# A hybrid attention and state-space layer on one core: the sample's scan chunk padded to 128 rows, its index heads taken in pairs

## The chip, the cores and the metric

The kernel runs on one core of a Trainium2 chip. The metric is device time in microseconds (us) of one execution, lower is better. A core has five engines that run their own instruction lists: TensorE (PE in the profile, with PEld for its weight loads), VectorE (DVE), ScalarE (ACT), GpSimd (POOL) and SyncE (SP), whose queue issues the transfers between main memory and on-chip memory. On-chip memory has 128 partitions ("rows" below); matmul results go to accumulator banks, which ScalarE and VectorE read out.

## What is computed

One layer of a streaming encoder, for a prompt of 512 tokens and a sample of 64 tokens with a cache of 512 keys. Both share all weights, so the kernel treats them as 576 tokens. Cut to what the change touches:

```python
# light indexer: scores over the keys, 8 heads, top k keys per query (sample: 144 of 576)
logits = einsum('thd,sd->ths', q_idx, k_idx) * 64 ** -0.5
score  = einsum('th,ths->ts', w, relu(logits))
idx    = top_k(score, k)            # attention then runs over these keys alone

# Mamba-2 scan, 32 heads in 8 groups, per chunk of tokens
decay  = exp(where(causal, acs_i - acs_j, -inf))
y_diag = einsum('ijg,ijgr,jgr,jgrp->igrp', cc @ bc, decay, dt, x)
y_off  = einsum('ign,igr,grpn->igrp', cc, exp(acs), h_prev)
y      = y_diag + y_off
```

Around this stand the conditioning (adaLN), one input projection, softmax attention over the chosen keys, a causal convolution, gates, an output projection and a SwiGLU feed-forward part.

## The kernel before

**How it is written and ordered.** The whole layer is recorded as a list of operations: each call on `pe`, `vec`, `act`, `pool` or `sync` becomes an `Op` of a `Plan` (line 229), with its reads and writes as dependences. `Plan.cost` (line 316) gives each operation a price, and `Plan.order` (line 363) simulates the five engines with these prices and a fixed delay between engines; whichever operation is ready first, by price and by place in the list, is put next into its engine's list. The order on every engine is therefore the result of the prices, and a changed price or a new operation can move others. All instructions are issued by one helper, so each has line 490 in the profile; tiles tell them apart. On the chip each engine works through its list strictly in order and waits with semaphores.

For a matmul the price depends on its form. Matmuls on rounded float32 (`F32R`) cost about their columns divided by 2.25 per ns; a plain float32 matmul has another price; and one with a `tile_position`, which places a 64- or 32-column weight tile in a part of the array, has (line 337)

```python
return (73 if o.shape[0] <= 32 else 8 + n) / 1e3, 0.10
```

with `n` the columns of the streamed operand.

**Precision.** Most products split both operands in a rounded high part and a rest (`wh`, `wl` of the weights, `hTh`, `hTl` of the activations) and add three matmuls. ScalarE rounds the weights (`wh`), VectorE forms the rest (`wl`). A plain float32 matmul, such as those of the scan, shows as two records in the profile.

**Stages.** Conditioning and normalization (about the first 80 us), input projection with the index part (80 to 260 us, lines 963 to 1118), attention of four key heads filled up with further columns of the projection (260 to 490), convolution and scan of eight groups interleaved with the last columns of the projection (490 to 850), branch projections with the rest of the conditioning (850 to 1010), output projection and feed-forward part (to the end).

**The index part (lines 1090 to 1118).** Block `b == 4` is the sample. Its queries lie in `qis` behind those of the prompt, head by head, 64 columns each; the weights of the heads lie in `wi`. For each of eight heads and each half of the 576 keys two matmuls (high part and rest of the keys `kis`) give `pix` in 64 rows, ScalarE applies the relu into a tile tagged `lg`, and VectorE multiplies by the head's weight and adds to `score4`. Then 18 rounds of `max` and `match_replace` on VectorE find the top 144 keys. Blocks 1 to 3 are the prompt's, with 128 rows.

**The scan (lines 1262 to 1311).** `chunk(g, c, xb, st)` computes chunk `c` of group `g`: chunks 0 to 3 are 128 prompt tokens each, chunk 4 is the 64 sample tokens. `bc` is loaded with the summed decay, GpSimd masks it into `dec`, ScalarE takes four exponentials, VectorE multiplies by `pc`, TensorE transposes the inputs, VectorE forms `xdt` and `xw`. Then, for each of four heads `h`,

```python
pe.matmul(o, xdt[:L, 64 * h:64 * h + 64], dec[:L, h, :L], start=True, stop=st is None,
          tile_position=(0, 64 * (h % 2)))
pe.matmul(o, st[:, 64 * h:64 * h + 64], cs[:, h, :L], start=False, stop=True,
          tile_position=(0, 64 * (h % 2)))
```

The first contracts over the `L` tokens of the chunk (64 for the sample), the second over the 128 state columns (`cs` is the decayed C, `st` the state). A further matmul of `xw` and `bt` gives the new state. `dec`, `xdt` and `xw` each have two buffers used in turn. `stage_a` (line 1327) is one projection tile (48 matmuls) and its convolution with the buffers `xc`, `cu` and `cth`; `stage_b` calls `chunk`, and for the sample it loads the state (`si`) first; `stage_c` normalizes a group. The loop at line 1383 interleaves them, and lets the conditioning's last two parts (`adr`, line 674) run in the last group.

**Memory.** Pools are opened and closed in a stack. The pools of the scan (`ssd`, line 1237, and `conv`, line 1239) take the place of attention's (`attn`, `attn2`), which hold among others the split probabilities `pth`, `ptl`, the copy `otmp` of an attention result (line 1175) and the sum `oT` (line 1226). The first write to a new tile waits for the last use of every old tile that lay there.

Of the kernel before, what the change touches and what calls it, by code (L numbers as in the profile page):

```python
# [5 lines left out]
F32 = mybir.dt.float32  # L6
# [7 lines left out]
P = 128  # L14
# [214 lines left out]
class Plan:  # L229
# [86 lines left out]
    def cost(self, op, outs, ins):  # L316
        e, fn = op.eng, op.fn
        o = outs[0] if outs else None
        if e == "sync":
            v = o if o is not None else ins[0]  # L320
            n = 4
            for k in v.shape:
                n *= k
            op.bytes = n
            return 0.06, 0.93
        n = _cols(o)
        if e == "tensor":
            op.mm = True
            if fn == "transpose":
                return 0.110, 0.10  # L330
            rhs = op.args[2]
            fast = rhs.dtype == F32R
            n = _cols(rhs)
            if fast:
                return (n / 2.25 + 4 if n > 128 else 110) / 1e3, 0.10
            if op.kw.get("tile_position") is not None:
                return (73 if o.shape[0] <= 32 else 8 + n) / 1e3, 0.10
            return ((4 * max(n, 128) / 2.4 if n > 1 else 190) + 5) / 1e3, 0.10
        psum = any(is_psum(v) for v in ins)
        if e == "scalar":  # L340
            t = n / 1.2 + (52 if psum else 92) + (96 if isinstance(op.kw.get("bias"), View) else 0)
            return (t + (93 if op.kw.get("accum_out") is not None else 0)) / 1e3, 0.19
        if e == "vector":
            if fn == "tensor_reduce":
                n = _cols(ins[0])
            if fn in ("max", "match_replace"):
                n = _cols(ins[0] if fn == "max" else o)
            if fn == "reciprocal":
                return (69 + 6.25 * n) / 1e3, 0.13
            src = sum(1 for v in ins if _cols(v) > 1)  # L350
            fast = src == 1 and fn in ("tensor_copy", "tensor_scalar") and not is_psum(o) and not psum
            column = fn in ("scalar_tensor_tensor", "tensor_scalar") and len(ins) > src
            more = 60 * column + 70 * (fn == "tensor_tensor_reduce")
            return (64 + 0.96 * more + n * (0.5 if fast else 1.0)) / 0.96e3, 0.13
        if fn == "memset":
            return (n * 0.5 + 60) / 1e3, 0.1
        if op.kw.get("op") == OP.pow or OP.pow in op.args:
            return (n * 165 + 300) / 1e3, 0.1
        per = {"tensor_copy": 3.33, "affine_select": 1.0, "tensor_tensor": 2.1}[fn]
        return (n * per + 150) / 1e3, 0.1  # L360
# [137 lines left out]
def build(tc, I, O):  # L498
# [476 lines left out]
    vec.tensor_copy(misc[:NS, 4, :], p[:NS, :104])  # L975
    wi = cp.tile([P, 5, 8], F32, name="wi")
    vec.tensor_scalar(wi, misc[:, :, 64:72], float(NIH ** -0.5), None, op0=OP.mult)

    ki = misc[:, :, 0:64]
    rope("ki", ki, cs2, 1, False)  # L980
# [109 lines left out]
    for b in (4, 1, 2, 3):  # L1090
        smp = b == 4
        n = T if smp else P * (b + 1)
        rows = NS if smp else P
        k0 = NP_ if smp else 0
        s = ix.tile([P, n], F32, name=f"score{b}")
        for h in range(NIH):
            q0 = 8 * NP_ + h * NS if smp else h * NP_ + b * P
            q = qis[:, q0:q0 + rows]
            for c0, cn in (((0, TH), (TH, TH)) if smp else ((0, n),)):
                ps = px(f"pix{b}_{h}_{c0}", "py")  # L1100
                for a in range(2):
                    pe.matmul(ps[:rows, :cn], q, kis[:, a, k0 + c0:k0 + c0 + cn], start=(a == 0), stop=(a == 1))
                r = ap_.tile([P, NP_], F32, name=f"relu{b}_{h}_{c0}", tag="lg", bufs=4)
                sv = s[:rows, c0:c0 + cn]
                act.activation(r[:rows, :cn], ps[:rows, :cn], AF.Relu, scale=float(HD ** -0.5))
                if h == 0:
                    vec.tensor_scalar(sv, r[:rows, :cn], wi[:rows, b, h:h + 1], None, op0=OP.mult)
                else:
                    vec.scalar_tensor_tensor(sv, r[:rows, :cn], wi[:rows, b, h:h + 1], sv, op0=OP.mult, op1=OP.add)
        if not smp:  # L1110
            pool.memset(s[0:64, n - 64:n], -1.0e38)
        m8 = ix.tile([P, 8], F32, name=f"m8_{b}")
        for r in range((TOPK_S if smp else TOPK_P) // 8):
            vec.max(m8[:rows], s[:rows, :n])
            vec.match_replace(s[:rows, :n], m8[:rows], s[:rows, :n], -3.0e38)
        vec.tensor_scalar(masks[b][:rows], s[:rows, :n], -2.0e38, NEG, op0=OP.is_gt, op1=OP.mult)
        if smp:
            vec.tensor_copy(masks[b][64:128], masks[b][0:64])
# [143 lines left out]
    def chunk(g, c, xb, st):  # L1262

        L = P if c < 4 else NS
        i0 = c * P
        nm = f"s{g}_{c}"
        h4 = lambda z: z[:L].rearrange("p (h d) -> p h d", h=4)
        bc = sd.tile([P, 4, P], F32, name=nm + "bc", tag="bc", bufs=2)
        sync.dma_start(bc[:, :, :L], acs_d[4 * g:4 * g + 4, i0:i0 + L][None].to_broadcast([P, 4, L]))
        dec = sd.tile([P, 4, P], F32, name=nm + "dec", tag="dec", bufs=2)  # L1270
        pool.affine_select(dec[:L, :, :L], bc[:L, :, :L], pattern=[[0, 4], [1, L]], compare_op=OP.is_ge, fill=NEG,
                           base=0, channel_multiplier=-1)
        for h in range(4):
            act.activation(dec[:L, h, :L], dec[:L, h, :L], AF.Exp, bias=nacs[:L, c, 4 * g + h:4 * g + h + 1])
        pt = px(nm + "xt")
        pc = pt[:, 384:512]
        pe.matmul(pc[:L, :L], xb[:, 2, i0:i0 + L], xb[:, 3, i0:i0 + L], start=True, stop=True)
        vec.tensor_tensor(dec[:L, :, :L], dec[:L, :, :L], pc[:L, None, :L].to_broadcast([L, 4, L]), OP.mult)
        for i in range(3):
            pe.transpose(pt[:L, P * i:P * i + P], xb[:, i, i0:i0 + L], ident)  # L1280
        xdt = sd.tile([P, 256], F32, name=nm + "xdt", tag="xdt", bufs=2)
        xw = sd.tile([P, 256], F32, name=nm + "xw", tag="xw", bufs=2)
        bt = sd.tile([P, P], F32, name=nm + "bt", tag="bt", bufs=2)
        for o, s in ((xdt, dtp), (xw, wst)):
            vec.tensor_tensor(h4(o), h4(pt[:, 0:256]), s[:L, c, 4 * g:4 * g + 4, None].to_broadcast([L, 4, HD]), OP.mult)
        act.activation(bt[:L], pt[:L, 256:384], AF.Copy)
        if st is not None:
            cs = sd.tile([P, 4, P], F32, name=nm + "cs", tag="cs", bufs=1)
            act.activation(bc[:, :, :L], bc[:, :, :L], AF.Exp)
            pool.tensor_tensor(cs[:, :, :L], bc[:, :, :L], xb[:, None, 3, i0:i0 + L].to_broadcast([P, 4, L]), OP.mult)  # L1290
        py = px(nm + "y", "py")
        for h in range(4):
            o = py[64 * (h % 2):64 * (h % 2) + 64, P * (h // 2):P * (h // 2) + L]
            pe.matmul(o, xdt[:L, 64 * h:64 * h + 64], dec[:L, h, :L], start=True, stop=st is None,
                      tile_position=(0, 64 * (h % 2)))
            if st is not None:
                pe.matmul(o, st[:, 64 * h:64 * h + 64], cs[:, h, :L], start=False, stop=True,
                          tile_position=(0, 64 * (h % 2)))
        ps = py[:, 256:512]
        pe.matmul(ps, bt[:L], xw[:L], start=True, stop=True)  # L1300
        new = sd.tile([P, 256], F32, name=nm + "h", tag="hst", bufs=4)
        if st is None:
            act.activation(new, ps, AF.Copy)
        else:
            pool.tensor_tensor(new.rearrange("p (h d) -> p h d", h=4), st.rearrange("p (h d) -> p h d", h=4),
                               edec[:, c, 4 * g:4 * g + 4, None].to_broadcast([P, 4, HD]), OP.mult)
            vec.tensor_tensor(new, new, ps, OP.add)
        for i in range(2):
            vec.scalar_tensor_tensor(xb[:, i, i0:i0 + L], xb[:, i, i0:i0 + L], dcol[:, 2 * g + i:2 * g + i + 1],
                                     py[:, P * i:P * i + L], op0=OP.mult, op1=OP.add)  # L1310
        return new
# [10 lines left out]
    so_p = O["ssm_prompt"][0, 0].rearrange("h p n -> (h p) n").rearrange("(g a p) n -> g p a n", a=2, p=P)  # L1322
    so_s = O["ssm_sample"][0, 0].rearrange("h p n -> (h p) n").rearrange("(g a p) n -> g p a n", a=2, p=P)

    xbs, sts = {}, {}

    def stage_a(g, i):
# [443 lines left out]
```

## Time and profile before

| what | value |
|---|---|
| median of 3 runs | 1446.85 us (1444.67 to 1447.4) |
| the profiled execution, whole | 1454.0 us |
| its span, first to last instruction | 1452.3 us |
| mean granted TensorE clock | 0.993 |
| TensorE busy, of the span | 1415.3 us |
| VectorE busy | 1078.2 us |
| ScalarE busy | 705.2 us |
| GpSimd busy | 211.1 us |
| moved by transfers | 179.73 MB |

The profile is of one execution. Lines of the timeline read: start in us, duration in us, engine, source line, operation, output tile <- input tiles, then for TensorE rows of contraction * columns of weights, then the output's partitions x elements, and xN for N merged instructions; in brackets stands the idle time ahead and who ended it. Rows of groups end in "busy us, mean ns of one | idle us before, and who ended it". Rows of stages give for each engine the busy time and in brackets the instructions, then the granted clock of TensorE, the share of busy transfer engines and GB/s. TensorE's matmuls are pipelined: their durations overlap, and what one costs is seen from the next one's start.

### The profile page before, as it was taken

Reading aid. Unit: us, or ns where it says so; the run is one execution under the profiler, and the core shown is the slowest. Engines: PE = TensorE matmul, PEld = TensorE weight load, DVE = VectorE, ACT = ScalarE, POOL = GpSimd, SP = SyncE. Lnnn points to the kernel's source line nnn. Section 1 sums busy time; section 2 is a strip of 40 time slices with the busy share of each in tenths; the row PEclk is TensorE's granted clock in tenths of the full one; section 3 lists DMA queues with packets and bytes.
Section 4 is the critical chain, followed back from the end, with each engine's and each line's share of the span. In section 5 each row is a group of like instructions: output and inputs, shape, how many; then the busy total and the mean of one; then the engine's idle time right before and its main releaser. Section 6 shows DMA issues by size and latency. Waiting matters only on the chain.

```text
span 1452.3 us, 27797 instructions
## 1 busy us (share of the span) xinstructions
PE 1415.3 (97%) x10865; PEld 1339.4 (92%) x10865; DVE 1078.2 (74%) x2123; ACT 705.2 (49%) x1482; POOL 211.1 (15%) x320
## 2 busy tenths in 40 slices
PE   7999999999999899999999899999999999999998
PEld 5889999999999699999998699999999999999998
DVE  4468999887877777778777578984699888874221
ACT  5335233556556656555555441123566666663221
POOL 1211001210200144444444210000000000000000
PEclk9999999999999999999999999999999999999999
DMA  9822346333332434344333857775513333324331
GB/s 281 227 73 76 84 112 163 94 84 89 109 92 77 129 99 108 100 112 111 84 88 96 280 171 238 230 229 170 165 44 102 88 99 92 102 70 137 112 107 28
DMA packets 262356, 179.73 MB, mean 124 GB/s; under 512 B 24272, under 2 KB 239472, under 8 KB 262224
## 3 DMA queue, kind: packets, MB, share of 16 engines
q1 hardware_dynamic: 262224, 177.95, 42.7%
q8 instruction: 85, 1.39, 0.4%
q14 instruction: 47, 0.39, 0.1%
HBM read 153.09 MB, written 24.83 MB: 123 GB/s over the span
## 4 chain that ended last, share of the span: by engine, by line
PE 84%; DVE 8%; DMA 5%; SPq 1%; ACT 1%; issue 1%; DVEq 0%; ACTq 0%
PE mm L490 60%; PE py L490 15%; PE px L490 8%; DMA adr<-in_w_ada 2%; DMA raw<-in_w_in 2%; DVE aacc L490 1%; SPq L490 1%; DVE wl L490 1%; DVE m L490 1%; DVE score L490 1%; DMA xt<-in_x_sample 1%; ACT wh L490 0%; DMA x2r<-x_d 0%; DVE P L490 0%; DVE e L490 0%
## 5 line engine op out<-in xcount | busy, mean ns | idle before, releaser
L490 ACT ACTIVATE wh<-raw 128x1024 fp32r<-128x1024 f32 (+2 forms) x159 | 156.6, 987 | 279.9 <-PE mm L490 222.4
L490 DVE TENSOR_TENSOR wl<-raw,wh 128x1024 fp32r<-128x1024 f32 (+1 forms) x137 | 169.0, 1236 | 100.6 <-ACT wh L490 97.8
L490 PE MATMUL mm<-hTl,wh 128*128 128x288 f32 (+1 forms) x1024 | 235.0, 304 | 0.0
L490 PE MATMUL mm<-hTh,wh 128*128 128x288 f32 (+1 forms) x1024 | 230.6, 302 | 1.7 <-ACT xc L490 1.5
L490 PE MATMUL mm<-hTh,wl 128*128 128x288 f32 (+1 forms) x1024 | 232.1, 301 | 0.0
L490 PEld LDWEIGHTS mm<-hTh,wh 128*128 128x128 f32 (+1 forms) x1024 | 166.7, 189 | 5.4 <-ACT xc L490 1.8
L490 PEld LDWEIGHTS mm<-hTl,wh 128*128 128x128 f32 (+1 forms) x1024 | 167.4, 189 | 4.0 <-issue 1.9
L490 PEld LDWEIGHTS mm<-hTh,wl 128*128 128x128 f32 (+1 forms) x1024 | 167.3, 189 | 2.7 <-issue 0.5
L490 DVE SCALAR_TENSOR_TENSOR cu<-xc,wc,cu 128x579 f32<-128x579 f32 x96 | 82.9, 868 | 4.0 <-ACT cu L490 3.5
L490 PE MATMUL mm<-fl,wh 128*128 128x288 f32 x352 | 80.6, 298 | 1.0 <-DVE fl L490 1.0
L490 PE MATMUL mm<-fh,wl 128*128 128x288 f32 x352 | 80.1, 298 | 0.9 <-DVE x2r L490 0.9
L490 PE MATMUL mm<-fh,wh 128*128 128x288 f32 x352 | 80.0, 297 | 0.0
L490 PE MATMUL mm<-wh,hTl 128*128 128x256 f32 x256 | 73.2, 286 | 0.0
L490 PE MATMUL mm<-wh,hTh 128*128 128x256 f32 x256 | 72.8, 286 | 0.0
L490 PE MATMUL mm<-wl,hTh 128*128 128x256 f32 x256 | 72.7, 284 | 0.0
L490 DVE SCALAR_TENSOR_TENSOR aacc<-adr,sil,aacc 128x512 f32<-128x512 f32 x84 | 58.7, 747 | 2.9 <-DMA adr<-in_w_ada 2.7
L490 ACT ACTIVATE P<-lg,mn 128x128 f32<-128x128 f32 (+4 forms) x72 | 41.8, 582 | 39.1 <-DVE mn L490 38.3
L490 PEld LDWEIGHTS mm<-fh,wl 128*128 128x128 f32 x352 | 58.2, 189 | 1.6 <-DVE x2r L490 1.4
L490 PEld LDWEIGHTS mm<-fl,wh 128*128 128x128 f32 x352 | 58.2, 189 | 1.6 <-DVE fl L490 1.4
L490 PEld LDWEIGHTS mm<-fh,wh 128*128 128x128 f32 x352 | 58.1, 189 | 0.1
L490 PE MATMUL mm<-yh,wl 128*128 128x288 f32 x256 | 56.8, 302 | 0.0
L490 PE MATMUL mm<-yh,wh 128*128 128x288 f32 x256 | 56.5, 300 | 0.0
(409 smaller groups left out, 3771.0 us busy)
## 6 DMA issues: line engine op xcount, KB each, us to landing
raw<-in_w_in SPq DMA_DIRECT2D x80, 512.0 KB, 4.2
adr<-in_w_ada SPq DMA_DIRECT2D x48, 512.0 KB, 5.2
rawu<-in_w_gate_up SPq DMA_DIRECT2D x22, 512.0 KB, 3.9
raw<-in_w_gate_up SPq DMA_DIRECT2D x22, 512.0 KB, 3.9
bc<-acs_d SPq DMA_DIRECT2D x32, 256.0 KB, 3.6
raw<-in_w_branch_ssm SPq DMA_DIRECT2D x16, 512.0 KB, 4.9
raw<-in_w_down SPq DMA_DIRECT2D x16, 512.0 KB, 3.7
gate_d<-sg SPq DMA_DIRECT2D x16, 288.0 KB, 4.8
```

The source lines that it names most:

```text
L490: getattr(engines[x.eng], x.fn)(*[real(a) for a in x.args], **{k: real(v) for k, v in x.kw.items()})
```

## The change

Three things are changed. The index part computes the sample's heads two at a time: the 64 columns of two neighbouring heads are one weight tile of 128 columns, so that even heads are summed in rows 0 to 63 of `score4` and odd heads in rows 64 to 127; a small tile `wi2` holds the head weights in that layout, and at the end ScalarE copies the odd half down and VectorE adds it. In the scan, the sample's chunk has `dec` and `xdt` tiles of its own, `decS` and `xdtS`, one buffer each, whose rows 64 to 127 are set to zero once at the start; the first of the two matmuls per head contracts over all 128 rows. The planner's price for matmuls with a `tile_position` and more than 32 columns of weights becomes 132 ns, whatever the streamed columns.

```diff
-                return (73 if o.shape[0] <= 32 else 8 + n) / 1e3, 0.10
+                return (73 if o.shape[0] <= 32 else 132) / 1e3, 0.10
...
+    wi2 = cp.tile([P, 4], F32, name="wi2")
+    for r in range(2):
+        vec.tensor_copy(wi2[64 * r:64 * r + 64], wi[0:NS, 4].rearrange("p (b r) -> p r b", r=2)[:, r])
...
-        for h in range(NIH):
-            q0 = 8 * NP_ + h * NS if smp else h * NP_ + b * P
-            q = qis[:, q0:q0 + rows]
+        for h in range(NIH // 2 if smp else NIH):
+            q0 = 8 * NP_ + h * P if smp else h * NP_ + b * P
+            q = qis[:, q0:q0 + P]
+            w1 = wi2[:, h:h + 1] if smp else wi[:, b, h:h + 1]
...
-                    pe.matmul(ps[:rows, :cn], q, kis[:, a, k0 + c0:k0 + c0 + cn], start=(a == 0), stop=(a == 1))
+                    pe.matmul(ps[:, :cn], q, kis[:, a, k0 + c0:k0 + c0 + cn], start=(a == 0), stop=(a == 1))
...
-        if not smp:
+        if smp:
+            odd = ap_.tile([P, T], F32, name="odd", tag="lg", bufs=4)
+            act.activation(odd[0:NS], s[NS:P, :], AF.Copy)
+            vec.tensor_tensor(s[0:NS, :], s[0:NS, :], odd[0:NS], OP.add)
+        else:
             pool.memset(s[0:64, n - 64:n], -1.0e38)
...
-        dec = sd.tile([P, 4, P], F32, name=nm + "dec", tag="dec", bufs=2)
+        dec = decS if c == 4 else sd.tile([P, 4, P], F32, name=nm + "dec", tag="dec", bufs=2)
...
-        xdt = sd.tile([P, 256], F32, name=nm + "xdt", tag="xdt", bufs=2)
+        xdt = xdtS if c == 4 else sd.tile([P, 256], F32, name=nm + "xdt", tag="xdt", bufs=2)
...
-            pe.matmul(o, xdt[:L, 64 * h:64 * h + 64], dec[:L, h, :L], start=True, stop=st is None,
+            pe.matmul(o, xdt[:, 64 * h:64 * h + 64], dec[:, h, :L], start=True, stop=st is None,
...
+    decS = sd.tile([P, 4, NS], F32, name="decS")
+    xdtS = sd.tile([P, 256], F32, name="xdtS")
+    pool.memset(decS[NS:P], 0.0)
+    pool.memset(xdtS[NS:P], 0.0)
```

The relu and the multiply-and-add of the index part work on 128 rows instead of 64 for the sample; all else is as before.

More of the change, by code (lines that the diff above doesn't have):

```diff
@@ L1101, in build @@
                 for a in range(2):
-                    pe.matmul(ps[:rows, :cn], q, kis[:, a, k0 + c0:k0 + c0 + cn], start=(a == 0), stop=(a == 1))
+                    pe.matmul(ps[:, :cn], q, kis[:, a, k0 + c0:k0 + c0 + cn], start=(a == 0), stop=(a == 1))
                 r = ap_.tile([P, NP_], F32, name=f"relu{b}_{h}_{c0}", tag="lg", bufs=4)
-                sv = s[:rows, c0:c0 + cn]
-                act.activation(r[:rows, :cn], ps[:rows, :cn], AF.Relu, scale=float(HD ** -0.5))
+                sv = s[:, c0:c0 + cn]
+                act.activation(r[:, :cn], ps[:, :cn], AF.Relu, scale=float(HD ** -0.5))
                 if h == 0:
-                    vec.tensor_scalar(sv, r[:rows, :cn], wi[:rows, b, h:h + 1], None, op0=OP.mult)
+                    vec.tensor_scalar(sv, r[:, :cn], w1, None, op0=OP.mult)
                 else:
-                    vec.scalar_tensor_tensor(sv, r[:rows, :cn], wi[:rows, b, h:h + 1], sv, op0=OP.mult, op1=OP.add)
-        if not smp:
+                    vec.scalar_tensor_tensor(sv, r[:, :cn], w1, sv, op0=OP.mult, op1=OP.add)
+        if smp:
[3 more added lines that the diff above has]
+        else:
             pool.memset(s[0:64, n - 64:n], -1.0e38)
```

## The prediction

> **What bounds the kernel now.** I read the first page from its top down, then a table of stages, then the waits of TensorE, and only then single instructions. The page says who is busy and what the chain that ended last is made of:
>
> ```profile
> span 1452.3 us, 27797 instructions
> ...
> PE 1415.3 (97%) x10865; PEld 1339.4 (92%) x10865; DVE 1078.2 (74%) x2123; ACT 705.2 (49%) x1482; POOL 211.1 (15%) x320
> ...
> PE 84%; DVE 8%; DMA 5%; SPq 1%; ACT 1%; issue 1%; DVEq 0%; ACTq 0%
> ```
>
> TensorE is busy for 97% of the span and holds 84% of the chain. An average can hide stages with other limits, so the next view cuts the span at the places that the change touches: the sample's index matmuls (110 to 126 us), the top-k after them (126 to 254), the end of attention (480 to 500), the scan (500 to 798), and the wait for data behind it (798 to 812).
>
> ```profile
> core 0: us, PE busy (x) PEld busy (x) DVE busy (x) ACT busy (x) POOL busy (x), PEclk, DMA share, GB/s
> 110.00:126.00 16.00, 16.00 (x128) 15.51 (x128) 13.93 (x29) 12.98 (x31) 1.54 (x1) 1.00 0.24 66
> 126.00:254.00 128.00, 127.67 (x970) 126.50 (x968) 123.73 (x270) 43.67 (x68) 9.62 (x7) 1.00 0.42 115
> 480.00:500.00 20.00, 16.75 (x76) 12.69 (x75) 14.19 (x29) 11.09 (x25) 1.94 (x13) 0.83 0.24 70
> 500.00:798.00 298.00, 297.82 (x2340) 269.66 (x2339) 232.56 (x446) 174.77 (x427) 134.06 (x229) 1.00 0.40 106
> 798.00:812.00 14.00, 9.71 (x93) 6.86 (x91) 7.28 (x12) 4.39 (x7) 1.70 (x2) 0.88 0.91 289
> ```
>
> In both stages that lose work TensorE never rests: 16.00 of 16 us and 297.82 of 298. VectorE is nearly as full behind the index scores (123.73 of 128) and has room in the scan (232.56 of 298). All that TensorE waited for in the scan, by the view of waits cut to 500 to 798 us, is one line:
>
> ```profile
> PE px L490 <- DVE dec L490: 0.2, 1, 0.2
> ```
>
> So a microsecond less of TensorE work in these stages is nearly a microsecond less of kernel, as long as nobody else becomes late.
>
> **The index part.** The sample had eight heads times two halves of the keys times two operand parts: 32 matmuls with 64 columns of weights. Two heads at a time make 16 with 128 columns. Their price is read from the timeline of TensorE, by starts, since the durations overlap:
>
> ```profile
> 112.90 0.43 PE L490 MATMUL py<-kis,qis 128*64 128x288 f32 x2
> 113.17 0.28 PE L490 MATMUL mm<-wh,hsS 128*128 128x256 f32 x1
> ```
>
> Two of them move the next matmul 0.27 us on, 0.135 us each. With 288 columns streamed in either form, 16 fewer are 16 x 0.135 = **2.2 us less TensorE work**. On VectorE eight of sixteen score operations go, and an addition over 576 columns and two small copies of head weights come. The nearest rows of the groups by shape are
>
> ```profile
> L490 DVE SCALAR_TENSOR_TENSOR score<-lg,wi,score 64x288 f32<-64x288 f32 x14 | 6.4, 507 | 0.6 <-ACT lg L490 0.6
> L490 DVE TENSOR_TENSOR m<-m,g 128x576 f32<-128x576 f32 x8 | 6.0, 755 | 0.0
> L490 DVE COPY misc<-px 64x104 f32<-64x104 f32 x1 | 0.2, 246 | 0.0
> ```
>
> which makes -8 x 0.507 + 0.755 + 2 x 0.246 = -2.8 us (128 rows instead of 64 are taken to cost the same time: a row is its own lane). VectorE, the other full engine of this stage, thus sheds as much as TensorE, and the end of the stage moves forward whichever of the two carries it. The new wait is a chain of last score, copy of the odd half on ScalarE, addition on VectorE. In the changed program's order VectorE has a score operation of the next block on each side of the addition, and ScalarE, 43.67 us busy of 128 in that stage, has evacuations behind its copy; TensorE has other products for all of that time; the chain of work shows one unbroken stretch of them:
>
> ```profile
> 190.96 62.78 PE mm L490 x471
> ```
>
> I take the new chain at nothing; with no cover it would cost about 1.5 us once (two operations of some 0.75 us).
>
> **The scan part.** This is the bigger term. The sample's chunk issues, per group, eight float32 matmuls with a column position, alternately `dec`/`xdt` with 64 rows of contraction and `cs`/state with 128 rows. Each appears as two records:
>
> ```profile
> 526.35 0.42 PE L490 MATMUL mm<-hTl,wh 128*128 128x288 f32 x2
> 526.61 0.43 PE L490 MATMUL mm<-hTh,wl 128*128 128x288 f32 x2
> 526.97 0.32 PE L490 MATMUL py<-dec,xdt 64*64 64x64 f32 x2
> 527.23 0.33 PE L490 MATMUL py<-cs,hst 128*64 128x64 f32 x2
> 527.48 0.33 PE L490 MATMUL py<-dec,xdt 64*64 64x64 f32 x2
> ...
> 529.02 0.70 PE L490 MATMUL py<-xw,bt 64*128 64x256 f32 x2
> ```
>
> From 526.97 to 529.02 the eight take 2.05 us: every change between 64 and 128 rows moves the next start by 0.26 us. A prompt chunk issues the same eight with 128 rows throughout and twice the columns:
>
> ```profile
> 535.12 0.45 PE L490 MATMUL py<-dec,xdt 128*64 128x128 f32 x4
> 535.39 0.40 PE L490 MATMUL py<-cs,hst 128*64 128x128 f32 x4
> 535.61 0.44 PE L490 MATMUL py<-dec,xdt 128*64 128x128 f32 x4
> 535.82 0.44 PE L490 MATMUL py<-cs,hst 128*64 128x128 f32 x4
> 536.19 0.70 PE L490 MATMUL py<-xw,bt 128*128 128x256 f32 x2
> ```
>
> 1.07 us for sixteen records, half of the sample's time for twice its columns. Padding the sample's contraction with zero rows puts all eight in the prompt's form, so 1.07 us bounds the new block from above. The lower end comes from one pair without a change in it, and the time of one load:
>
> ```profile
> L490 PEld LDWEIGHTS py<-dec,xdt x320: 129/136/137, 520.4 to 842.4; 128*64 128x64 f32 x128, 64*64 64x64 f32 x32
> 526.97 0.19 PEld L490 LDWEIGHTS py<-dec,xdt 64*64 64x64 f32 x2 [0.17 <-DVE xw L490]
> ```
>
> Two loads of 0.136 us span 0.19 us, so the second starts 0.054 us after the first. With twice the columns a record takes 0.108 us; sixteen in two column halves that run beside each other are 8 x 0.108 = 0.86 us, and 0.21 us of the prompt's 1.07 is entry and exit. The same with 0.054 gives 8 x 0.054 + 0.21 = 0.64 us. Between 0.64 and 1.07 I take the middle, 0.85: half the columns must shorten something, but the weights that each record loads are the prompt's. A group then saves 1.2 us (0.98 to 1.41), and eight groups **9.6 us** (7.8 to 11.3). The `xw`/`bt` matmul keeps its 64 rows; its own entry and exit stay as they are. VectorE, with 65 us free in this stage, loses nothing by the shorter block.
>
> Here a rule speaks against the change. The Trainium skill, "TensorE: Matmul & The Clock Gate", Part 3, "What overlaps and what doesn't", says that a weight load overlaps matmuls in flight only when its row group differs; after padding all eight share all rows. The trace differs: it shows 1.07 us for sixteen records in one row group, where load and stream one after the other would need 16 x 0.108 = 1.73 us even with 64 columns.
>
> **What the change moves besides.** Two tiles of 1 KB per partition at the head of the scan's pool push the convolution's input buffers 2 KB up. In the built programs the first of them, `xc`, lay on attention's probability splits; it now lies also on `otmp`, which the last `oT` addition reads. Today the first evacuation into `xc` begins at 492.76, before that addition ends, and the second one waits for it:
>
> ```profile
> 492.76 0.78 ACT L490 ACTIVATE xc<-mm 128x288 f32<-128x288 f32 x3
> 493.71 0.78 ACT L490 ACTIVATE xc<-mm 128x288 f32<-128x288 f32 x3 [0.17 <-DVE oT L490]
> 492.77 0.85 DVE L490 TENSOR_TENSOR oT<-py,otmp 64x256 f32<-64x256 f32 x2 [1.21 <-ACT otmp L490]
> 493.59 0.85 PE L490 MATMUL mm<-hTh,wh 128*128 128x288 f32 x2 [1.48 <-ACT xc L490]
> ```
>
> TensorE waits 1.48 us for that first evacuation. In the changed program both evacuations wait for `oT`, so the first starts when the second does now: 493.71 - 492.76 = **0.95 us more idle TensorE**, once (0 at best, if the addition is done sooner; some 2 at worst, if the pause prolongs the stretch of lower clock, 0.83 in this window). The cover it loses is real: nothing else is queued on TensorE ahead of that accumulator. The two zero fills stand on GpSimd ahead of the convolution's fills and wait for tiles long read; GpSimd is idle there. `decS` and `xdtS` take the sample out of the two-buffer rings of `dec` and `xdt`, which can only release GpSimd's selections earlier.
>
> The planner's own price for these matmuls (72 to 132 ns with 64 columns) and the new operations make it lay out the order anew from the index part on. The lists of SyncE differ only by transfers that change places with near neighbours. After the scan TensorE still stands before the same load:
>
> ```profile
> 807.33 1.08 PE L490 MATMUL py<-adr,sil 128*32 128x128 f32 x16 [2.99 <-DMA adr<-in_w_ada]
> ```
>
> That load is issued when earlier matmuls of TensorE free its buffer, and the window's other loads when the last `hTh` matmul has run, so this stall moves forward with TensorE and neither grows nor shrinks; I count 0, with 1 us either way.
>
> **The sum** is -2.2 - 9.6 + 0.95 = -10.9 us (rounded). The profiled execution took 1454.0 us, 1.7 of them outside its span of 1452.3; from it the changed kernel would take 1443.1. It stands 7.15 us above the median of the three runs, 1446.85, and the forecast goes by that median: 1446.85 - 10.9 = **1436.0 us**.
>
> **The rivals.**
>
> *The loads are not hidden.* If a weight load does wait for the matmuls in flight of its rows, a record costs load plus stream, 0.054 + 0.054 us, the block 1.73 us, and a group saves 0.32: -2.2 - 8 x 0.32 + 0.95 = -3.8, 1443.0 us. For it: no row shows eight 64-column matmuls in a row with 128 rows. Against it: the prompt's 1.07 us. This is the time that the quoted rule of the Trainium skill gives.
>
> *The change does not do what it says.* The 0.26 us per pair could belong to short matmuls that add into the same accumulator, not to the change of rows. Then only the index part and the seam count: -1.25 us, 1445.6 us, which cannot be told from no change. Against it: the pair within one operation adds into the same accumulator too, and moves on after 0.054 us.
>
> *Slower: ScalarE is blocked in the scan.* In the changed order ScalarE's four exponentials on `decS` and that on `bc` stand earlier than before, ahead of weight roundings and of the evacuations of TensorE's accumulators; they wait, by way of GpSimd's selection, for the sample's `bc` load. TensorE has two accumulators, and one product is 48 matmuls of 0.13 us (the two rows at 526.35 and 526.61), 6.4 us. So a blocked ScalarE costs nothing up to 6.4 us and every microsecond beyond it stops TensorE. It turns the sign from 10.9 / 8 = 1.4 us beyond that, at blocks of 7.8 us per group; blocks of 9 us would give -10.9 + 8 x 2.6 = +9.9, 1456.8 us. For it: the order is laid out anew, and no row shows the new one. Against it: ScalarE is busy 174.77 of 298 us, and the load lands in less than that by far:
>
> ```profile
> bc<-acs_d SPq DMA_DIRECT2D x32, 256.0 KB, 3.6
> ```
>
> **How the numbers follow.** Forecast 0.70, loads not hidden 0.08, no effect of the rows 0.07, slower 0.12; 0.03 is left for gains beyond the forecast's own ends. Those ends are, with the block at 0.64 us, no cost at the seam and 1 us less stall behind the scan, -2.2 - 11.3 - 1 = -14.5 (1432.4), and with the block at 1.07, 2 at the seam and 1 us more stall, -2.2 - 7.8 + 3 = -7.0 (1439.9). The range runs from 1431.5, a little below the first, for the runs' own spread, to 1443.5, which takes in the rival of the loads; it holds some 0.79. Faster or slower means by more than 0.2%, 2.9 us, about what a measurement of this kernel tells from no change: faster 0.81, same 0.07, slower 0.12.
>
> **What would show it.** In the profile after, 16 rows `kis`/`qis` with 128x288; in each group the start of `xw`/`bt` or of the next product 0.64 to 1.07 us after the first `decS`/`xdtS`, and no step of 0.26 us between pairs. TensorE's wait for `xc` near 490 us should be about 2.4 us. Wrong would be: a block near 1.7 or 2.05 us; waits of TensorE for ScalarE inside the scan; or a shorter scan whose gain is found again as a longer wait for `adr`.

## The result and the profile after

The changed kernel takes **1434.0 us** (median of four runs, 1431.16 to 1435.6) beside 1446.68 for the kernel before (four runs, 1444.67 to 1447.4): a ratio of 0.9912, 95% interval 0.9893 to 0.9932, 12.7 us less. The forecast was 1436.0 (10.9 less), with a range of 1431.5 to 1443.5. A second comparison on another occasion, told below, gave 0.9898 (0.9881 to 0.9915), again with a median of 1434.0.

The first page of the changed kernel's profile, the lines that answer to those of before (busy times, and the chain that ended last):

```profile
span 1433.3 us, 27708 instructions
...
PE 1396.6 (97%) x10849; PEld 1326.3 (93%) x10849; DVE 1081.6 (75%) x2118; ACT 702.6 (49%) x1475; POOL 217.7 (15%) x322
...
PE 86%; DVE 7%; DMA 3%; ACT 1%; issue 1%; SPq 1%; POOL 0%; ACTq 0%; DVEq 0%
```

The span fell by 19.0 us and TensorE's busy time by 1415.3 - 1396.6 = 18.7. Its idle time is 36.7 us after 37.0, but these are not the same waits: ahead of the first index matmul it fell from 16.4 to 12.9 us, and in the stages behind that it rose by 3.2 in sum (0.6 in the index stage, 0.9 at the seam, 1.2 in the scan, 0.8 at the end, and 0.3 less in the others together). TensorE still holds the chain.

19.0 is more than the 12.7 of the medians, so a part of it belongs to the two executions and not to the change. To find it, the span is cut at instructions that both kernels have (differences of their starts in the timeline of TensorE, us). Beside the two first profiles stands a second one of each kernel, told below (TensorE busy 1413.5 and 1398.7 us, idle 34.1 and 34.3):

```
stage (first to last)                     before  again   after   again
start to the first index matmul           112.90  108.05  107.09  108.03
first to last index matmul                 77.42   77.43   75.10   75.09
to the last product of attention (ptl)    301.29  301.27  301.13  301.48
seam, to the scan's first px<-xb           23.92   23.45   25.22   25.21
scan, to the last px<-ident,rows          335.60  335.76  325.62  324.79
branches, to the first mm<-mh             141.39  141.64  139.66  139.14
to the first feed-forward mm<-fh          302.21  302.18  302.20  302.24
to the last mm<-fh,wh                     152.13  152.38  151.09  151.06
to the end                                  5.44    5.44    6.19    6.06
```

Most stages repeat within 0.3 us; the changed kernel's scan and branches and before's seam differ by 0.5 to 0.8. Only the first one is off by more, and it holds the same work in the same order in both kernels: before's first execution spent 4.85 us more there than its second, 3.4 of them as idle time of TensorE. That is why the forecast did well to go by the median and not by the profiled execution. Taking means of the two columns, the change gives -2.3 (index), +1.5 (seam), -10.5 (scan), -2.1 (branches), -1.2 (feed-forward) and +0.7 (end): -13.9 us, of the size of the measured 12.7 and 13.9.

*Index.* The matmuls' row in the view of the tile, and one pair in the timeline of TensorE:

```profile
L490 PE MATMUL py<-kis,qis x64: 274/334/497, 107.1 to 182.4; 128*128 128x288 f32 x16, 128*128 128x256 f32 x16, 128*128 128x384 f32 x16, 128*128 128x512 f32 x16
```

```profile
113.84 0.42 PE L490 MATMUL py<-kis,qis 128*128 128x288 f32 x2
114.10 0.28 PE L490 MATMUL mm<-wl,hTh 128*128 128x256 f32 x1
```

Sixteen of 288 columns where there were 32, and two of them still move the next one on by 0.26 us. TensorE's idle time in this stage is 1.0 us after 0.3: a wait of 0.3 us for VectorE's `wl` and a second one as long for ScalarE's `lg` are new.

*Scan.* The sample's block of one group, in the timeline of TensorE, and the weight loads of the same block:

```profile
600.82 0.29 PE L490 MATMUL mm<-hTl,wh 128*128 128x288 f32 x1
601.04 0.34 PE L490 MATMUL py<-decS,xdtS 128*64 128x64 f32 x4
601.20 0.29 PE L490 MATMUL py<-cs,hst 128*64 128x64 f32 x4
601.32 0.33 PE L490 MATMUL py<-decS,xdtS 128*64 128x64 f32 x4
601.43 0.33 PE L490 MATMUL py<-cs,hst 128*64 128x64 f32 x4
601.70 0.70 PE L490 MATMUL py<-xw,bt 64*128 64x256 f32 x2
602.33 0.49 PE L490 MATMUL px<-xb 128*128 128x128 f32 x2
```

```profile
601.03 0.20 PEld L490 LDWEIGHTS py<-decS,xdtS 128*64 128x64 f32 x4 [0.16 <-issue]
601.14 0.21 PEld L490 LDWEIGHTS py<-cs,hst 128*64 128x64 f32 x4
601.26 0.25 PEld L490 LDWEIGHTS py<-decS,xdtS 128*64 128x64 f32 x4
601.38 0.25 PEld L490 LDWEIGHTS py<-cs,hst 128*64 128x64 f32 x4
```

The block lasts 601.70 - 601.04 = 0.66 us, in all eight groups 0.66 or 0.67, where it lasted 2.05 or 2.06. A step of four records takes 0.11 to 0.16 us; only the last one, ahead of another form of tile, takes 0.27. The loads keep the matmuls' pace.

*What TensorE waits for in the scan* (view of waits, 498 to 860 us), and the two loads behind it in the timeline:

```profile
PE py L490 <- DMA adr<-in_w_ada: 4.0, 2, 3.0
PE mm L490 <- ACT oh L490: 1.5, 1, 1.5
```

```profile
790.68 0.65 PE L490 MATMUL py<-adr,sil 128*32 128x128 f32 x16 [3.00 <-DMA adr<-in_w_ada]
813.52 0.64 PE L490 MATMUL py<-adr,sil 128*32 128x128 f32 x16 [1.04 <-DMA adr<-in_w_ada]
```

No wait for ScalarE but the one for `oh` at the end, 1.30 us before and 1.5 now. The stall at `adr` is 3.00 us after 2.99, and a second one of 1.04 us is new (0.67 in the second profile, whose first one is 2.58).

*Seam.* TensorE's first matmul after its wait, ScalarE's first evacuation, and two rows from the slower stretch that follows:

```profile
486.25 0.53 PE L490 MATMUL mm<-hTh,wh 128*128 128x288 f32 x2 [2.43 <-ACT xc L490]
...
488.10 0.68 PE L490 MATMUL mm<-hTh,wh 128*128 128x288 f32 x2
488.58 0.68 PE L490 MATMUL mm<-hTl,wh 128*128 128x288 f32 x2
```

```profile
485.42 1.45 ACT L490 ACTIVATE xc<-mm 128x288 f32<-128x288 f32 x6 [0.97 <-DVE oT L490]
```

The evacuations now wait for `oT`, and TensorE's wait is 2.43 us after 1.48: 0.95 more, to the hundredth what was forecast. From 488.10 to 490.98 a pair takes 0.48 us instead of 0.27; before's seam has such a stretch too.

### The profile page after: what moved, and what is told of

It is laid out like the page before. It is cut to its first block, busy times and chain, and to the rows that moved or that the text cites. A ratio compares the mean times of both kernels' runs of the same rounds, so it can differ in the third digit from the quotient of the medians.

```text
span 1433.3 us, 27708 instructions
## 1 busy us (share of the span) xinstructions
PE 1396.6 (97%) x10849; PEld 1326.3 (93%) x10849; DVE 1081.6 (75%) x2118; ACT 702.6 (49%) x1475; POOL 217.7 (15%) x322
## 3 DMA queue, kind: packets, MB, share of 16 engines
q8 instruction: 85, 1.39, 0.4%
## 4 chain that ended last, share of the span: by engine, by line
PE 86%; DVE 7%; DMA 3%; ACT 1%; issue 1%; SPq 1%; POOL 0%; ACTq 0%; DVEq 0%
PE mm L490 63%; PE py L490 15%; PE px L490 9%; DMA adr<-in_w_ada 2%; DVE score L490 1%; DVE wl L490 1%; DVE m L490 1%; SPq L490 1%; DVE aacc L490 1%; DMA raw<-in_w_in 0%; DVE P L490 0%; DVE e L490 0%; ACT wh L490 0%; DMA xt<-in_x_prompt 0%; DVE ptl L490 0%
## 5 line engine op out<-in xcount | busy, mean ns | idle before, releaser
L490 DVE SCALAR_TENSOR_TENSOR cu<-xc,wc,cu 128x579 f32<-128x579 f32 x96 | 87.1, 911 | 4.0 <-ACT cu L490 3.2
```

Of the source, the lines that this page charges most:

```text
L490: getattr(engines[x.eng], x.fn)(*[real(a) for a in x.args], **{k: real(v) for k, v in x.kw.items()})
```

## The experiments

**The scan part alone**, with the planner's new price. Against the changed kernel, cut:

```diff
-        for h in range(NIH // 2 if smp else NIH):
-            q0 = 8 * NP_ + h * P if smp else h * NP_ + b * P
+        for h in range(NIH):
+            q0 = 8 * NP_ + h * NS if smp else h * NP_ + b * P
...
-            odd = ap_.tile([P, T], F32, name="odd", tag="lg", bufs=4)
```

> The scan part alone, with the sample's index heads one at a time as before. If the eight sample blocks carry the gain as the changed kernel's profile shows them (2.05 us to 0.66 us each, 11.1 us in all) and the seam costs its 0.95 us, this run is 10.2 us below the kernel before: 1436.5 us, and the eight blocks are again 0.66 us. If a good part of the gain came from the whole order being laid out anew together with the index part, it is nearer 1440 us or above.

Measured: 1437.32 us, ratio 0.9927 (0.9908 to 0.9945), 10.2 us below the 1447.56 of the kernel before in that comparison. The blocks are 0.66 or 0.67 us, the scan stage 324.33 us, the index stage 77.42 as before. The scan part does not need the index part. The new price is in this run; what it is worth by itself is told below.

**The index part alone.** Against the kernel before, only the hunks at `wi2` and in the index part, cut:

```diff
+    wi2 = cp.tile([P, 4], F32, name="wi2")
...
+        for h in range(NIH // 2 if smp else NIH):
```

> The index part alone, with the scan as before. By the forecast's first term, 16 matmuls of 0.135 us fewer, 2.2 us: 1444.5 us. If VectorE's addition and the new wait before the sample's top-k eat that, 1446.7 us. The blocks of the scan stay at 2.05 us and TensorE's wait for xc at 1.5 us.

Measured: 1443.3 us beside 1447.56, ratio 0.9975 (0.9962 to 0.9988): 4.3 us by the medians, 3.6 by the ratio. The index stage takes 75.09 us after 77.42, 2.3 us less. The other differences are further on, where not one operation was changed: the seam is 1.1 us shorter (no stretch of low clock there in this execution), the scan 0.7 longer, the branches 2.4 shorter and the feed-forward stage 1.2 (with 0.5 given back at the end).

**The planner's price alone.** Against the kernel before:

```diff
-                return (73 if o.shape[0] <= 32 else 8 + n) / 1e3, 0.10
+                return (73 if o.shape[0] <= 32 else 132) / 1e3, 0.10
```

> The kernel before with nothing changed but the planner's price of the matmuls with a column position, so that only the order of the work moves. By the forecast the new order by itself is worth nothing: 1446.7 us, within 1 us. The rival is that a part of the gain is the order's: the terms that the profile confirms give 10 to 11 of the 12.7 us, so this run would be 1.5 to 2 us faster, some 1445 us.

Measured: 1442.98 us beside 1447.56, ratio 0.9956 (0.9939 to 0.9973). The order alone is worth some 4.6 us (6.4 by the ratio), and the expectation of nothing was wrong. Seven of its eight sample blocks are as long as before, and the last one is split by other products; TensorE's timeline of one:

```profile
607.31 0.33 PE L490 MATMUL py<-dec,xdt 64*64 64x64 f32 x2
607.56 0.33 PE L490 MATMUL py<-cs,hst 128*64 128x64 f32 x2
...
609.10 0.33 PE L490 MATMUL py<-cs,hst 128*64 128x64 f32 x2
609.36 0.70 PE L490 MATMUL py<-xw,bt 64*128 64x256 f32 x2
```

The scan stage nevertheless takes 331.30 us after 335.7. If one counts in TensorE's timeline how often a row's form of tile (rows and columns) differs from that of the row ahead of it, this stage has 217 changes after 239 in the kernel before. So 22 changes fewer go with 4.3 us less, 0.20 us for each; in the scan-only run 57 fewer (182) go with 11.3 us less, 0.20 us again. The time is indeed gone at the changes: from start to start, without waits, the stage's steps across a change sum to 43.8 us after 48.9, those without one to 283.4 after 282.4.

**Grouping instead of padding.** Against the kernel before, rows of 64 kept:

```diff
+        for hs in ((0, 1), (2, 3)) if c == 4 else ((0,), (1,), (2,), (3,)):
+            for h in hs:
+                pe.matmul(o[h], xdt[:L, 64 * h:64 * h + 64], dec[:L, h, :L], ...)
+            for h in hs if st is not None else ():
+                pe.matmul(o[h], st[:, 64 * h:64 * h + 64], cs[:, h, :L], ...)
```

> The kernel before, the sample's eight matmuls issued two dec, two cs, two dec, two cs, instead of turn by turn; 64 rows stay. If each change between 64 and 128 rows costs time (seven inside the block make up the 1.39 us between 2.05 and 0.66, 0.20 us each), three changes leave a block of 0.66 + 3 x 0.20 = 1.26 us and the run is 8 x 0.79 = 6.3 us faster: 1440.4 us. If a matmul of 64 rows is slow by itself, whatever stands next to it, the block stays at 2.05 us and the time at 1446.7 us.

Measured: 1438.71 us beside 1447.56, ratio 0.9936 (0.9919 to 0.9953), 8.9 us less. TensorE's timeline of one group:

```profile
603.26 0.33 PE L490 MATMUL py<-dec,xdt 64*64 64x64 f32 x4
603.52 0.34 PE L490 MATMUL py<-cs,hst 128*64 128x64 f32 x4
603.78 0.33 PE L490 MATMUL py<-dec,xdt 64*64 64x64 f32 x4
604.04 0.34 PE L490 MATMUL py<-cs,hst 128*64 128x64 f32 x4
604.31 0.70 PE L490 MATMUL py<-xw,bt 64*128 64x256 f32 x2
```

The block is 1.05 us. It still has 64 rows, and the same sixteen records; only the changes are fewer. Each of the four steps takes 0.26 us with four records in it, as each of the eight steps took 0.26 with two. So it is neither the 64 rows nor the records that cost here, but the change itself: what stands between two changes takes 0.26 us, be it two records or four. The expected 1.26 had charged the records a second time. Over the scan stage 32 changes fewer (207) go with 8.4 us less, 0.26 us for each, so the 0.20 of the two other runs is an average and no constant. Grouping gets much of what padding gets in the block (1.00 of 1.39 us) without zero rows or own buffers.

**The seam, other places for the convolution's tiles.** Against the changed kernel, `u` and `th` are made ahead of `xc`:

```diff
+        n = T + 3
+        u = sda.tile([P, n], F32, name=name + "u", tag="cu", bufs=2)
+        th = sda.tile([P, n], F32, name=name + "th", tag="cth", bufs=1)
         xc = sda.tile([P, 6 + T], F32, name=name + "xc", tag="xc", bufs=2)
```

> The changed kernel with the convolution's two other tiles (u and th) laid out ahead of xc, so that xc lies behind attention's otmp and its first evacuation waits for nobody. If TensorE's wait for xc is what the seam costs, its 2.43 us goes (1.48 of it was there before, 0.95 came with the change): 1431.6 us. If u or th, which now lie on otmp, wait in its place and TensorE with them, 1434.0 us.

Measured: 1433.41 us beside 1448.25, ratio 0.9905 (0.9885 to 0.9925); the time cannot be told from the changed kernel's. The stage can: 24.18 us after 25.2. Its wait in TensorE's timeline:

```profile
490.20 0.85 PE L490 MATMUL mm<-hTh,wh 128*128 128x288 f32 x2 [1.48 <-ACT xc L490]
```

1.48 us, as in the kernel before. So the 0.95 us were the new place of `xc`. The 1.48 are no wait for a place: in this run ScalarE copies attention's last result into `otmp` from 488.75 to 489.34 and starts the first evacuation at 489.37, without a wait between them. The expected 2.4 us were too many for that reason.

**Padding `xw` and `bt` as well.** Against the changed kernel:

```diff
-        pe.matmul(ps, bt[:L], xw[:L], start=True, stop=True)
+        pe.matmul(ps, bt, xw, start=True, stop=True)
...
+    pool.memset(xwS[NS:P], 0.0)
+    pool.memset(btS[NS:P], 0.0)
```

> The changed kernel with xw and bt of the sample padded with zero rows as well, so that no 64-row matmul is left in the sample's chunk. In the changed kernel's profile the next matmul after the sample's xw/bt starts 0.63 us behind it, after a prompt chunk's 0.35 us. If the change of rows is the cost wherever it stands, the eight groups save 8 x 0.28 = 2.2 us: 1431.8 us. If the change of column form that is left (64 to 128 columns) costs the same alone, 1434.0 us.

Measured: 1432.57 us beside 1448.25, ratio 0.9897 (0.9878 to 0.9915), 1.4 us below the changed kernel's median and not clear of it. TensorE's timeline:

```profile
603.89 0.34 PE L490 MATMUL py<-cs,hst 128*64 128x64 f32 x4
604.15 0.70 PE L490 MATMUL py<-xwS,btS 128*128 128x256 f32 x2
604.69 0.38 PE L490 MATMUL px<-xb 128*128 128x128 f32 x2
```

The step ahead of it is still 0.26 us (64 to 128 columns is a change too) and the one behind it 0.54 us after 0.63. That is 0.1 us a group, 0.7 us in all. The expected 0.28 came from setting a row with a transposition behind it beside a prompt's row with a product behind it: ahead of a transposition a prompt chunk's `xw`/`bt` takes 0.54 too, as this place of the kernel before shows:

```profile
521.01 0.70 PE L490 MATMUL py<-xw,bt 128*128 128x256 f32 x2
521.55 0.38 PE L490 MATMUL px<-ident,si 128*128 128x128 f32 x2
```

Rows are to be compared with the same neighbours only. (The scan stage is 322.88 us after 325.62 and, in the second profile, 324.79; 1.0 of the first difference is less wait at `adr`.)

**The old price in the changed kernel.**

```diff
-                return (73 if o.shape[0] <= 32 else 132) / 1e3, 0.10
+                return (73 if o.shape[0] <= 32 else 8 + n) / 1e3, 0.10
```

> The changed kernel with the planner's price of before (72 ns instead of 132). In the order that it gives TensorE changes between whole and partial tiles 5 times less than in the changed kernel (176 for 181). At 0.2 us for a change, as the scan-only and the price-only runs give it (11.3 us for 57 changes, 4.3 us for 22), it is 1.0 us faster: 1433.0 us. If the gain that the new price brought on top of the kernel before is in the changed kernel too, it is 4.3 us slower: 1438.3 us.

Measured: 1432.94 us beside 1448.25, ratio 0.9901 (0.9883 to 0.9919). It is not slower, so the gain that the price brings to the kernel before is no part of this change's gain; whether it is 1 us faster the runs do not tell. Its order also moves 14 of TensorE's records from the branches into the scan stage, so the two are to be read together: 462.6 us beside 465.3 and 463.9 in the changed kernel's profiles. The wait for `adr` is gone from it, with one of 2.2 us for `xb` in its place.

**The kernel before once more.**

> The kernel before once more, for its profile alone. If the time that its first profile shows ahead of the index part (first index matmul at 112.90 us, at 107.1 to 111.0 in the five other profiles, which issue the same work in the same order up to there) is that execution's own, it now comes to 111 us or less and the span is nearer 1446 us than 1452.3. If it belongs to the order of before, 112.9 us again.

Measured: one run of 1449.27 us, span 1447.6. Its first index matmul in TensorE's timeline:

```profile
108.05 0.42 PE L490 MATMUL py<-kis,qis 128*64 128x288 f32 x2
108.31 0.28 PE L490 MATMUL mm<-wh,hsS 128*128 128x256 f32 x1
```

108.05 us. The 4.85 us are the first execution's own. The later stages repeat within 0.5 us (table above).

**The changed kernel once more.**

> The changed kernel once more, beside the kernel before on one chip. The parts that the profiles show add to 2.3 us (index) + 10.0 us (scan, with what its own order and the load of adr take back) - 1.3 us (seam) = 11.0 us; if nothing else differs, its ratio is 0.9924. If the 12.7 us of the first comparison are the change's own, 0.9912 again. In the profile: eight blocks of 0.66 us, a wait for xc of 2.43 us.

Measured: 1434.0 us beside 1447.85, ratio 0.9898 (0.9881 to 0.9915). 0.9924 lies outside this interval and inside the first one, which speaks for somewhat more than the 11.0 us of the parts but does not settle it. The stages fit that: the branches and the feed-forward part are shorter again (139.14 and 151.06 us).

**All three edits together** (`xw`/`bt` padded, tiles re-placed, old price; their diffs stand above).

> The changed kernel with three edits together: xw and bt of the sample padded too, u and th laid out ahead of xc, and the planner's old price. If they add up as the profiles of the three single runs show them (8 x 0.28 us at the xw/bt matmuls, 1.0 us between attention and scan, 1.0 us for five changes of tiles less), it is 4.2 us faster than the changed kernel: 1429.8 us. If the load of adr behind the scan or the waits near it take back what the scan gives, it is no faster than the two that were fastest alone: 1432.7 us.

Measured: 1430.84 us (five runs, 1424.02 to 1433.24) beside 1447.85, ratio 0.9872 (0.9852 to 0.9892), on the same chip as the run just told. 3.2 us below the changed kernel by the medians, with intervals that still touch. It has the lowest median here. Scan (323.08) and seam (24.27) are 2.1 and 0.9 us shorter than the changed kernel's; scan and branches together, as under the old price, are 458.9 us beside 465.3 and 463.9. The sum of 4.2 is neither confirmed nor excluded by the times.

## Why the prediction was right, point by point

**Bound.** Right: TensorE's time at work fell by what the span fell by, 18.7 of 19.0 us in the first profiles and 14.8 of 14.5 in the second.

**Index part**, -2.2 forecast, -2.3 for the stage in every one of the profiles that have it. The 288-column records themselves give 2.0 of it (from start to start, 4.4 us before and 2.4 after). The stage also leaves three product records to the next one and has 0.6 us more idle time, so that the match to 0.1 us is partly luck; the new waits were taken at nothing and are not quite that.

**Scan block**, 0.85 us forecast, 0.66 measured: the mechanism was right and the size too small, 1.39 a group for 1.2. The middle of the range was taken because the weights that a record loads did not shrink. The row with two loads 0.054 us apart already spoke for the lower end, 0.64; the steps of four weight loads begin 0.11 to 0.12 us apart like those of the matmuls, so the loads do not hold them up. The stage gained 10.5 us, not 8 x 1.39 = 11.1, as the second stall at `adr` (1.04 and 0.67 us) is new; the forecast had allowed 1 us there.

**Seam**, +0.95 forecast. The wait itself grew by exactly that, and placing `xc` elsewhere took it away. The stage grew by 1.5 us. The clock is not what makes the difference: behind the wait the granted clock was half in the kernel before as well as in the changed one (view by windows, the clock is the number behind POOL's count), with six slow pairs in each:

```profile
493.16:496.57 3.41, 2.98 (x12) 2.98 (x13) 1.74 (x4) 2.66 (x8) 0.87 (x8) 0.50 0.57 180
```

```profile
488.10:490.98 2.88, 2.88 (x13) 2.88 (x13) 2.88 (x5) 0.27 (x1) 0.00 (x0) 0.50 0.84 207
```

One product record more, some 0.13 us, stands in the changed kernel's stage; what makes up the other 0.4 is open, and before's own two profiles differ by 0.47 there. With the index part alone there was no half clock, after the same wait of 1.48 us as in the kernel before, and the stage took 22.61 us:

```profile
487.00:493.00 6.00, 4.52 (x28) 3.83 (x29) 3.12 (x6) 3.66 (x9) 1.11 (x10) 1.00 0.39 114
```

**The order at nothing.** Right for this change as far as the price goes, but the assumption was not safe. The price alone moved the kernel before by 4.6 us, so an order laid out anew is not worth nothing in general. In the changed kernel the count of changes in the scan fell by 57 (239 to 182), of which 56 are the seven inside each of eight blocks: it has next to nothing from elsewhere.

**What was not foreseen**, -2.1 us in the branches and -0.5 in the feed-forward part with the end. In the branches the work is the same: TensorE is busy for 138.2 us there in both profiles of the changed kernel, and for 139.7 and 139.8 in those of the kernel before, where the clock falls once behind the wait for `aacc`. The rows of both kernels, and the windows around that place in steps of 3.41 us:

```profile
908.12 0.43 PE L490 MATMUL px<-aacc,pick 128*32 128x128 f32 x8 [1.39 <-DVE aacc L490]
...
909.95 0.68 PE L490 MATMUL mm<-yh,wh 128*128 128x288 f32 x2
```

```profile
906.18:909.59 3.41, 2.02 (x25) 1.22 (x24) 3.41 (x6) 1.06 (x1) 0.00 (x0) 1.00 0.89 269
909.59:913.00 3.41, 3.41 (x15) 3.40 (x16) 2.20 (x4) 0.78 (x2) 0.00 (x0) 0.50 0.67 192
```

```profile
891.11 0.43 PE L490 MATMUL px<-aacc,pick 128*32 128x128 f32 x8 [1.32 <-DVE aacc L490]
```

```profile
887.11:890.52 3.41, 2.69 (x21) 2.45 (x19) 1.90 (x4) 1.04 (x1) 0.00 (x0) 1.00 1.00 285
890.52:893.93 3.41, 2.82 (x30) 2.26 (x31) 3.41 (x6) 0.02 (x1) 0.00 (x0) 1.00 0.43 127
```

These steps follow the clock. Between 200 us and the last 8 us, the twelve profiles of this case hold 31 stretches of half clock. Each lasts 3.41 us (one lasts three times that), and within an execution they start whole multiples of 3.41 us apart. Each follows a step in which TensorE was idle for at least 1.0 us. Here before's wait of 1.39 us lies in one step, and the next one runs at half clock; the changed kernel's 1.32 is cut into 0.72 and 0.59, and the clock stays. So the same wait can cost or not, by where it falls. That is not the whole rule: in the grouped run the wait of 1.48 us for `xc` lies in one step too, and no half clock follows.

The fall costs 1.5 us of the 2.1; the rest is idle time, 1.7 and 1.9 us before and 1.4 and 0.9 after. Neither is shown to be the change's: the scan-only, price-only and grouped runs have 138.2 us of work and no fall there either, without the index part. In the feed-forward part a wait for `x2r` is gone in the kernels with the index part; the kernel before, then the changed kernel:

```profile
1322.22 0.55 PE L490 MATMUL px<-ident,x2r 128*128 128x128 f32 x3 [0.48 <-DVE x2r L490]
```

```profile
1302.81 0.49 PE L490 MATMUL px<-ident,x2r 128*128 128x128 f32 x3
```

All five profiles without the index part have this wait (0.31 to 1.02 us), none with it has. Why the index part should matter that far on was not tried and stays open.

**The total.** It fits better than its terms. The scan gave 0.9 us more than forecast and the seam took 0.6 more, so that the three terms come to -11.3 for -10.9; the 2.6 us of the branches and the feed-forward part were in no term.

**The rivals.** *Loads not hidden* is refuted: 0.66 us against 1.73. *No effect of the rows* is refuted by the block and by grouping. *ScalarE blocked* did not come about: no row of TensorE's waits in the scan names it before `oh`.

## What to carry to other kernels

Where short matmuls of different tile forms take turns on TensorE, count the changes of form, not the columns: in this scan each cost 0.20 to 0.26 us, and padding, grouping by form and even a lucky order all gained by having fewer of them. Not every change in the printed form counts: in the index stage of the kernel before, records of 288 columns change between 128*64 and 128*128 and still move the next one on by some 0.13 us (108.05 to 108.31 above for two). Those have no `tile_position`; whether that is the reason was not tried. Cut the profiles of two kernels at instructions that both have and compare stage by stage: a difference in a stage that holds the same work in the same order (here up to 5 us at the start) is the execution's, and a second profile of the kernel before tells how large that is. When a size lies between two bounds and one row shows the pace itself, take the bound that goes with that row, not the middle.

## What the runs showed of the hardware

- Between two changes of tile form a step takes 0.26 us whether two or four records of 64 columns stand in it; without a change four records take 0.11 to 0.16. The Trainium skill says in "TensorEngine Tiling (Array Packing)", section "Key Properties", that changing the tiling mode drains TensorE; a cost of 0.20 to 0.26 us for each change fewer in the scan fits that, though no view shows the drain itself.
- The Trainium skill's rule that a weight load overlaps matmuls only in another row group ("TensorE: Matmul & The Clock Gate", Part 3, "What overlaps and what doesn't") does not hold for these: sixteen loads and sixteen matmuls over all 128 rows, in two column halves, take 0.66 us together. The prompt's block, with the same sixteen loads and twice the streamed columns, takes 1.07; by that, as an estimate, 0.41 of the 0.66 goes with the columns and 0.25 is left for all else, the loads included.
- TensorE's granted clock falls to half for 3.41 us at a time, at places that lie whole multiples of 3.41 us apart within an execution. It fell after waits of 1.39 us (branches), 1.48 and 2.43 us (seam), and after waits of 1.32 (branches) and 1.48 us (seam) in other executions it did not.
